# A two-layer decoder with a top-2 expert layer: experts ordered by size on the chip, the two smallest with both halves of 64 tokens side by side

## The chip, the cores and the metric

The kernel runs on one core of a Trainium2 chip. The metric is the device time of one execution in microseconds (us). The kernel before took 1534.06 us, the median of 3 runs (1532.68 to 1534.2). The engines are named as in the profile: PE (matrix products), PEld (its weight loads), DVE (vector), ACT (scalar), POOL (GpSimd) and SP, whose queue issues the DMAs that bring the weights.

## The reference, cut to what matters

256 tokens of width 1024 pass two layers. Each has a mixer (attention and a short convolution side by side), a feed-forward part and a gated embedding. The feed-forward part is dense in layer 0; in layer 1 every token goes to the two best of eight experts:

```python
def swiglu(x, w1, w3, w2):
    return (jax.nn.silu(x @ w1) * (x @ w3)) @ w2

logits = (xt @ router_w).astype(jnp.float32)
top_vals, top_idx = lax.top_k(logits, TOP_K)
gates = jax.nn.softmax(top_vals, axis=-1)
...
for e in range(N_EXPERTS):
    out = out + combine[:, e:e + 1] * swiglu(xt, w1[e], w3[e], w2[e])
```

An expert's w1 and w3 are 1024 x 3584, its w2 is 3584 x 1024, all fp32. With the inputs given, experts 0 to 7 get 53, 69, 62, 74, 73, 57, 68 and 56 tokens.

## The kernel before

**Precision.** An fp32 operand is split into a high part (a cast to the matrix format) and a low part (the rest). A product of two split operands is three products, low by high, high by low and high by high, summed in one PSUM tile (`mm3`, L180 to L183).

**Weights.** They come in DMAs of 1 MB, 128 partitions by 2048, into raw buffers (`load`, L82 to L86; 14 buffers, tag `raw`). `split` (L88 to L96) makes of each piece of PART = 1024 columns a high part `wh` (ACT, L94) and a low part `wl` (DVE, L95); there are NPART = 5 buffers for each. `prepare` splits ahead of use, `loads` issues DMAs ahead of that, and `weights` hands the parts to PE in the order of `plan`. A split can start when PE has used up a buffer of the five; a DMA when DVE has read a raw buffer.

**The expert layer** takes the time from 514 to 1499.5 us. `Route` computes the logits, ranks them by small DVE operations (L731 to L747) and numbers the tokens of each expert. `Gather` picks an expert's tokens (up to 128) by products with a 0/1 matrix `sl` (L809), two experts at a time, then scales them by the norm's gain and splits them (`scaled_split`, L210 and L211). Each expert goes through NB = 7 blocks of 512 hidden columns. In a block, `expert_up` makes two tiles `pe` of 128 tokens by 512 (48 products), ACT applies the Silu (`s`, L848), DVE multiplies (`m`, L851), `hidden_T` transposes `m` on PE (L586) and splits it into `th` (ACT, L590) and `tl` (DVE, L591), and `expert_down` adds 24 products to the two tiles `y`, one block later. So a block has six DMAs of weights, twelve pieces and 72 products of 512 columns. At an expert's end `y` is split (L877, L878) and `combine` brings it back to the tokens by products `pc` (L885, L886), which DVE adds, weighted with the gate, in two halves (L887). If an expert has more than 128 tokens, a second part of the program (`over`) runs after; it doesn't here.

**Order.** The order of PE's instructions is written out by hand everywhere, that of ACT and DVE too within the expert layer. An engine that waits holds up all that stands behind it.

The products of the second layer's embedding (`ppp`, 24 of them) stand in the last expert, in block EMB = 2.

Of the kernel before, what the change touches and what calls it, by code (L numbers as in the profile page):

```python
# [7 lines left out]
F32 = mybir.dt.float32  # L8
# [13 lines left out]
NE = 8  # L22
# [3 lines left out]
PART = 1024  # L26
NPART = 5
LOADS = (9, 14)
EMB = 2
EPS = 1e-6  # L30

# [13 lines left out]
def trunk(ctx: ExitStack, tc: tile.TileContext, a, out):  # L45
# [4 lines left out]
    rawp = pool("rawp", 14)  # L50
# [46 lines left out]

    def emb(l):

        return [(a["pT"][l].rearrange("p k s -> p (k s)"), S), (a["w_p"][l], D)]  # L100
# [3 lines left out]
    for l in range(2):  # L104
        plan += [(a["w_in"][l, j, hf], 512 if j < 3 else S) for j in range(6) for hf in range(2)]
        plan += [(a["w_o"][l, n, i], 512) for i in range(2) for n in range(2)]
        for e in range(1 if l == 0 else NE):
            up = [a[n] if l == 0 else a[n][e] for n in (("d_w1", "d_w3") if l == 0 else ("m_w1", "m_w3"))]
            dn = a["d_w2"] if l == 0 else a["m_w2"][e]
            plan += [[(w[b, hf], 512) for w in up for hf in range(2)] + [(dn[b, hf], D) for hf in range(2)]  # L110
                     + (emb(l) if (l, e, b) in ((0, 0, NB - 2), (1, NE - 1, EMB - 1)) else [])
                     for b in range(NB)]
        plan += [(a["w_g"][l, n, hf], 512) for n in range(2) for hf in range(2)]
# [19 lines left out]
    def loads(upto):  # L133

        for i in range(len(ready), min(upto, len(parts))):
            (src, n), c = parts[i]
            if i not in raws:
                w = src.shape[-1]
                raw = load(src, w, 2 if i < 4 else 1)
# [78 lines left out]
    class Transposed:  # L218
# [19 lines left out]
        def rest(self):  # L238
            self.step(4)
            self.step(6)  # L240
            if ahead[0] < NPART:
                ahead[0] = NPART
                prepare(used[0] - 2 + NPART)
# [63 lines left out]
    def mixer(l, xt, after):  # L307

        with tc.tile_pool(name="att", bufs=2) as ap, tc.tile_pool(name="att1", bufs=1) as a1:
            if l == 0:  # L310
# [5 lines left out]
                ready.extend([wp.tile([P, 2, 512], F32R, tag=n, name=n) for n in ("wh", "wl")] for _ in range(2))  # L316
# [5 lines left out]
                for k in range(KD):  # L322
                    scaled_split(xh[:, k, :], xl[:, k, :], xr[:, k, :], par[:, G_MIX + k:G_MIX + k + 1])
                    if k < 4:
                        wh, wl = [x[:, k % 2, :] for x in ready[k // 2]]
# [257 lines left out]
    def hidden_T(m, fp):  # L583
# [3 lines left out]
        th = fp.tile([P, 4, P], F32R, tag="th", name="th")  # L587
        tl = fp.tile([P, 4, P], F32R, tag="tl", name="tl")
# [77 lines left out]
    class Parts:  # L666


        def __init__(self):
            self.x = {}  # L670
# [5 lines left out]
        def part(self, n, t):  # L676
            self.half(n)
            hh, hl = self.x[n][:, 0, t, :], self.x[n][:, 1, t, :]
            hn = h[t][:, n * 512:(n + 1) * 512]
            nc.scalar.copy(hh, hn)  # L680
            nc.vector.tensor_sub(hl, hn, hh.bitcast(F32))

        def block(self, k, t):

            return [self.x[k // 4][:, i, t, k % 4 * P:(k % 4 + 1) * P] for i in (1, 0)]

    class Route:


        def __init__(self, l):  # L690
            self.l = l
            self.rs = TokenRstd()
            self.split = Parts()
# [31 lines left out]
        def choose(self, mp, rp):  # L725
# [22 lines left out]

            pp = tp.tile([P, 512], F32, tag="t", name="ppos")
# [454 lines left out]
```

## Time and profile before

| what | us |
|---|---|
| median of 3 runs | 1534.06 |
| the profiled execution | 1535.4 |
| its span | 1533.4 |
| PE busy | 1512.3 (99%) |
| DVE busy | 1280.8 (84%) |
| ACT busy | 1093.1 (71%) |
| DMA, share of 16 engines' span | 76.3% |

The span is the profiled execution from its first to its last instruction; 2.0 us lie around it. Busy PE says that a product was under way or queued in the array, not that it ran at full rate: products overlap, so the distance between the starts of two is what one costs, not the length of its row.

### The profile page before, as it was taken

The page shows a single profiled execution, that of the slowest core. Times are in us where ns is not written, and L with a number is a line of the kernel's source. Part 1 is how long each engine was busy: PE and PEld are TensorE (multiplying, and loading weights), DVE is VectorE, ACT ScalarE, POOL GpSimd, SP SyncE. Part 2 cuts the span into 40 slices and gives each one's busy share as a digit, 9 for nine tenths or more (in the row PEclk, how much of TensorE's full clock was granted, in tenths as well). Part 3 has the DMA queues.
Part 4 walks back from the last instruction along what each step waited for, and adds up shares of the span by engine and source line. Part 5 has one row for each costly group of instructions (what it writes and reads, how often), then busy time and mean ns, then how long its engine had stood idle before and what let it go on. Part 6 is the DMA issues. An engine that isn't in the chain of part 4 may idle for free.

```text
span 1533.4 us, 19945 instructions
## 1 busy us (share of the span) xinstructions
PE 1512.3 (99%) x7249; PEld 1255.3 (82%) x7249; DVE 1280.8 (84%) x1553; ACT 1093.1 (71%) x1470; POOL 92.7 (6%) x96
## 2 busy tenths in 40 slices
PE   7999999999999999999999999999999999999998
PEld 5888888887898788888888888888888888888886
DVE  6896555556788799999899899999999999999895
ACT  4756444446676678878878778777877887877874
POOL 3440000000242000000000000000000000000000
PEclk9999999999999899999999999999999999999999
DMA  9656555343444799897999998999998899989960
GB/s 360 253 208 231 192 192 171 138 164 111 169 186 168 284 378 352 329 357 283 361 375 370 356 362 329 380 398 378 356 358 333 312 359 380 375 335 338 355 264 30
DMA packets 64043, 445.84 MB, mean 291 GB/s; under 512 B 7104, under 2 KB 9024, under 8 KB 10432
## 3 DMA queue, kind: packets, MB, share of 16 engines
q1 hardware_dynamic: 63936, 444.48, 76.3%
q8 instruction: 59, 0.97, 0.2%
q14 instruction: 48, 0.39, 0.1%
HBM read 443.40 MB, written 1.05 MB: 290 GB/s over the span
## 4 chain that ended last, share of the span: by engine, by line
PE 93%; DVE 3%; ACT 1%; POOL 1%; DMA 1%; issue 1%; SPq 0%; DVEq 0%; ACTq 0%
PE pe L181 13%; PE pe L183 13%; PE pe L182 13%; PE y L183 8%; PE y L182 8%; PE y L181 8%; PE p L182 3%; PE p L183 3%; PE p L181 3%; PE pt L586 2%; PE pj L181 1%; PE pj L183 1%; PE pj L182 1%; DVE wl L95 1%; PE pg L809 1%; PE po L181 1%
## 5 line engine op out<-in xcount | busy, mean ns | idle before, releaser
L95 DVE TENSOR_TENSOR wl<-raw,wh 128x1024 fp32r<-128x1024 f32 (+1 forms) x999 | 1016.2, 1057 | 178.8 <-ACT wh L94 166.4
L94 ACT CAST wh<-raw 128x1024 fp32r<-128x1024 f32 (+1 forms) x1000 | 881.1, 913 | 238.0 <-PE pe L183 78.2
L181 PE MATMUL pe<-wh,xl 128*128 128x512 f32 x896 | 350.6, 391 | 0.0
L183 PE MATMUL pe<-wh,xh 128*128 128x512 f32 x896 | 349.2, 390 | 0.0
L182 PE MATMUL pe<-wl,xh 128*128 128x512 f32 x896 | 348.7, 389 | 0.0
L181 PE MATMUL y<-wh,tl 128*128 128x512 f32 x560 | 226.2, 404 | 0.0
L182 PE MATMUL y<-wl,th 128*128 128x512 f32 x560 | 220.8, 394 | 0.5 <-DVE wl L95 0.5
L183 PE MATMUL y<-wh,th 128*128 128x512 f32 x560 | 220.9, 394 | 0.0
L183 PEld LDWEIGHTS pe<-wh,xh 128*128 128x128 f32 x896 | 168.2, 188 | 36.3
L182 PEld LDWEIGHTS pe<-wl,xh 128*128 128x128 f32 x896 | 168.2, 188 | 35.9 <-DVE wl L95 0.4
L181 PEld LDWEIGHTS pe<-wh,xl 128*128 128x128 f32 x896 | 168.2, 188 | 35.1
L183 PEld LDWEIGHTS y<-wh,th 128*128 128x128 f32 x560 | 105.1, 188 | 25.2
L182 PEld LDWEIGHTS y<-wl,th 128*128 128x128 f32 x560 | 105.3, 188 | 22.7 <-DVE wl L95 1.2
L181 PEld LDWEIGHTS y<-wh,tl 128*128 128x128 f32 x560 | 105.3, 188 | 21.6 <-ACT wh L94 0.2
L181 PE MATMUL p<-wh,xl 128*128 128x512 f32 x224 | 87.8, 392 | 0.0
L183 PE MATMUL p<-wh,xh 128*128 128x512 f32 x224 | 87.3, 390 | 0.0
L182 PE MATMUL p<-wl,xh 128*128 128x512 f32 x224 | 87.2, 389 | 0.0
L590 ACT CAST th<-pt 128x512 fp32r<-128x512 f32 x70 | 40.9, 586 | 41.8 <-PE pt L586 41.8
L95 POOL TENSOR_TENSOR wl<-raw,wh 128x1024 fp32r<-128x1024 f32 x1 | 2.4, 2380 | 990.2 <-ACT wh L94 990.2
L181 PE MATMUL pu<-xh,wl 128*128 128x256 f32 x192 | 55.7, 290 | 0.0
L182 PE MATMUL pu<-xl,wh 128*128 128x256 f32 x192 | 54.3, 283 | 0.0
L183 PE MATMUL pu<-xh,wh 128*128 128x256 f32 x192 | 54.2, 283 | 0.0
(201 smaller groups left out, 1545.2 us busy)
## 6 DMA issues: line engine op xcount, KB each, us to landing
raw<-m_w SPq DMA_DIRECT2D x336, 1024.0 KB, 6.0
raw<-d_w SPq DMA_DIRECT2D x42, 1024.0 KB, 4.8
raw<-w_in SPq DMA_DIRECT2D x22, 1024.0 KB, 6.7
raw<-w_o SPq DMA_DIRECT2D x8, 1024.0 KB, 5.2
raw<-w_g SPq DMA_DIRECT2D x8, 1024.0 KB, 4.8
raw<-w_p SPq DMA_DIRECT2D x2, 1024.0 KB, 4.8
raw<-w_in SPq DMA_DIRECT2D x4, 256.0 KB, 5.0
raw<-w_in SPq DMA_DIRECT2D x2, 512.0 KB, 8.5
```

What stands on the lines that cost most here:

```text
L94: nc.scalar.copy(wh[:, cs], raw[:, cs])
L95: eng.tensor_sub(wl[:, cs], raw[:, cs], wh[:, cs].bitcast(F32))
L181: nc.tensor.matmul(ps, ll, rh, start=start, stop=False)
L182: nc.tensor.matmul(ps, lh, rl, start=False, stop=False)
L183: nc.tensor.matmul(ps, lh, rh, start=False, stop=stop)
L586: nc.tensor.transpose(pt[:, c * P:(c + 1) * P], m[:, c * P:(c + 1) * P], ident)
L590: nc.scalar.copy(th, pv)
L809: nc.tensor.matmul(pts[kk], src, self.sl[:, t, :, :].rearrange("p i s -> p (i s)"), start=(i == 0), stop=(i == 2 * NT - 1))
```

## The change

**Sizes.** A piece is now 2048 columns (a whole DMA), with 3 buffers for `wh` and `wl` in place of 5 of half the size, and 13 raw buffers in place of 14.

**Order of the experts.** Expert 0 goes first as before. `places` ranks the other seven by their count of tokens, with some 26 small DVE operations in the first block, and loads the order into registers of SP; the weights of places 1 to 7 are fetched from an address that a register gives (`expert_w`). Positions, selections and gates are brought into the same order (`by`). Here 56 and 57 tokens are the two smallest; they take places 2 and 5.

**Two small experts.** They have 64 slots. The high part of 64 tokens and their low part stand side by side in one stationary operand of 128 columns (`xs`). An up tile then takes two products per slice, by `wl` and by `wh` (L932), in place of three. Its partitions 0 to 63 then hold the high parts' share, 64 to 127 the low parts'; ACT copies the tile to SBUF (`f`, L938), and `fold` adds the two by one product with a matrix `both` (L945, fp32 on both sides, 64 x 512). The down part takes two products too (L986, L987); its halves are added in `combine`, where `iota2` gives both halves a slot. Each small expert runs with a large one, block by block in turn (`SETS`).

**Transposes.** Those of a block come in the next step: on PE after the first up piece (`turn`), DVE's low part after the second (`low`), behind `back`, which brings a finished expert to the tokens.

**Gathers.** h is scaled by the gain and split once (`gains`, `part`), then high and low parts are gathered separately and ACT alone takes them out of PSUM. The embedding's products go into the route (`fill`). The experts' results are added to h itself.

On PE, the end of an up part and the start of a down part; `pe` is the up tile, `y` the down tile, `xh` and `xl` the tokens. Before, any block:

```order
L181 MATMUL pe<-wh,xl 128x512
L182 MATMUL pe<-wl,xh 128x512
L183 MATMUL pe<-wh,xh 128x512
L181 MATMUL y<-wh,tl 128x512
L182 MATMUL y<-wl,th 128x512
L183 MATMUL y<-wh,th 128x512
```

After, a small expert's up part and the large one's down part behind it:

```order
L932 MATMUL pe<-wl,xs 128x512
L932 MATMUL pe<-wh,xs 128x512
L945 MATMUL pf<-f,both 64x512
L206 MATMUL y<-wh,tl 128x512
L207 MATMUL y<-wl,th 128x512
L208 MATMUL y<-wh,th 128x512
```

The up tile gets its second of two products where it got its third of three, and the fold's product stands between it and the down part.

On ACT, blocks of the expert layer; `th` is the transposed hidden tile's high part. Before, two blocks:

```order
L94 CAST wh<-raw 128x1024 x6
L590 CAST th<-pt 128x512
L94 CAST wh<-raw 128x1024 x6
L848 ACTIVATE s<-pe,rslot 128x512
L94 CAST wh<-raw 128x1024 x6
```

After, one step of a small and one of a large expert (the first Silu, `s<-pf`, is the small one's):

```order
L101 CAST wh<-raw 128x2048 x5
L972 CAST th<-pt 128x512
L101 CAST wh<-raw 128x2048
L938 COPY f<-pe 128x512
L101 CAST wh<-raw 128x2048 x2
L938 COPY f<-pe 128x512
L952 ACTIVATE s<-pf,rslot 64x512
L101 CAST wh<-raw 128x2048 x3
L972 CAST th<-pt 128x4x64
L101 CAST wh<-raw 128x2048
L952 ACTIVATE s<-pe,rslot 128x512
```

Half as many casts of twice the width, and two copies `f` between those of the small expert.

On DVE, the end of one expert and the start of the next; the numbers tell tiles apart. Before:

```order
L878 TENSOR_TENSOR y_6081<-y_5147,y_6081 128x512
L878 TENSOR_TENSOR y_6081<-y_5148,y_6081 128x512
L95 TENSOR_TENSOR wl_6090<-raw_6087,wh_6089 128x1024
L95 TENSOR_TENSOR wl_6100<-raw_6087,wh_6099 128x1024
L95 TENSOR_TENSOR wl_6112<-raw_6109,wh_6111 128x1024
L95 TENSOR_TENSOR wl_6122<-raw_6109,wh_6121 128x1024
L887 SCALAR_TENSOR_TENSOR hout_6133<-pc_6134,gate_4953,h0_97 128x512
L887 SCALAR_TENSOR_TENSOR hout_6133<-pc_6138,gate_4953,h1_98 128x512
L95 TENSOR_TENSOR wl_6146<-raw_6143,wh_6145 128x1024
L95 TENSOR_TENSOR wl_6156<-raw_6143,wh_6155 128x1024
L887 SCALAR_TENSOR_TENSOR hout_6133<-pc_6165,gate_4953,h0_97 128x512
L887 SCALAR_TENSOR_TENSOR hout_6133<-pc_6169,gate_4953,h1_98 128x512
```

After:

```order
L1008 TENSOR_TENSOR y_5640<-y_4798,y_5640 128x512
L1008 TENSOR_TENSOR y_5640<-y_4799,y_5640 128x512
L102 TENSOR_TENSOR wl_5649<-raw_5646,wh_5648 128x2048
L102 TENSOR_TENSOR wl_5679<-raw_5676,wh_5678 128x2048
L1017 SCALAR_TENSOR_TENSOR h0_97<-pc_5692,gatev_4583,h0_97 128x512
L1017 SCALAR_TENSOR_TENSOR h1_98<-pc_5696,gatev_4583,h1_98 128x512
L978 TENSOR_TENSOR tl_5700<-pt_5660,th_5665 128x512
L102 TENSOR_TENSOR wl_5706<-raw_5703,wh_5705 128x2048
L1017 SCALAR_TENSOR_TENSOR h0_97<-pc_5717,gatev_4583,h0_97 128x512
L1017 SCALAR_TENSOR_TENSOR h1_98<-pc_5721,gatev_4583,h1_98 128x512
```

Two casts' worth of `wl` still stand between the split of `y` and the first add, and the low part `tl` of the hidden tile `pt_5660`, transposed before, now comes behind the adds of `pc_5692` and `pc_5696`. The pool `tp` has two PSUM tiles for `pt` and `pc`.

The diff, cut to its core:

```diff
-PART = 1024
-NPART = 5
-LOADS = (9, 14)
-EMB = 2
+PART = 2048
+NPART = 3
+LOADS = (9, 10)
+HALF = 64
+SETS = ((0,), (1, 2), (3,), (4, 5), (6,), (7,))
+SMALL = (2, 5)
+RANK = (0, 3, 1, 4, 5, 2, 6, 7)
+STEPS = [(e, b) for es in SETS for b in range(NB) for e in es]
...
-    rawp = pool("rawp", 14)
+    rawp = pool("rawp", 13)
...
+    chosen = {}
+    class expert_w:
+        def __init__(self, name, e, b, hf):
+            self.at, self.shape = (name, e, b, hf), (P, 2048)
+
+        def ap(self):
+            name, e, b, hf = self.at
+            if e == 0:
+                return a[name][0][b, hf]
+            return a[name][bass.ds(chosen[e], 1), b, hf].rearrange("o p n -> (o p) n")
...
+        def gains(self):
+            self.g = rawp.tile([P, 2 * D], F32, tag="raw", name="gain")
+            for n in range(2):
+                pt = tp.tile([P, 512], F32, tag="t", name="pgn")
+                for k in range(4):
+                    nc.tensor.matmul(pt[:, k * P:(k + 1) * P],
+                                     par[:, self.g0 + n * 4 + k:self.g0 + n * 4 + k + 1].broadcast_to([P, P]), ident,
+                                     start=True, stop=True)
+                nc.scalar.copy(self.g[:, n * 512:(n + 1) * 512], pt)
...
+            ns = slice(n * 512, (n + 1) * 512)
+            hg = self.g[:, D + t * 512:D + (t + 1) * 512]
+            nc.vector.tensor_mul(hg, h[t][:, ns], self.g[:, ns])
+            nc.scalar.copy(hh, hg)
+            nc.vector.tensor_sub(hl, hg, hh.bitcast(F32))
...
+            fill()
...
+        def places(self):
...
+            nc.vector.tensor_copy(c8, self.n8)
+            nc.vector.memset(c8[:, 0:1], -1.0)
+            nc.vector.tensor_tensor(same, row(c8), col(c8), op=ALU.is_equal)
+            nc.vector.tensor_mul(same, same, elow)
+            nc.vector.tensor_tensor(less, row(c8), col(c8), op=ALU.is_lt)
+            nc.vector.tensor_add(less, less, same)
+            rank = rp.tile([P, NE], F32, tag="rank8", name="rank8")
+            nc.vector.reduce_sum(rank, less, axis=AX.X)
+            nc.vector.tensor_tensor(at, row(rank), col(self.q8), op=ALU.is_equal)
+            nc.vector.reduce_sum(order, tmp, axis=AX.X)
+            self.order = mp.tile([P, NE], I32, tag="orderi", name="orderi")
+            nc.vector.tensor_copy(self.order, order)
...
+            for e in range(1, NE):
+                chosen[e] = nc.values_load(self.order[0:1, e:e + 1], engines=[mybir.EngineType.SP],
+                                           min_val=0, max_val=NE - 1)
...
+            self.x = xp.tile([P, KD, S], F32R, tag=tag, name="xe")
+            if self.n > 1:
+                self.xs = rawp.tile([P, KD, P], F32R, tag="raw", name="xs")
+
+        def step(self, k, pls=((tp, "t"), (tp, "t"))):
+            w = P + (self.n - 1) * HALF
+            for kk, (pl, tag) in enumerate(pls):
+                pt = pl.tile([P, 512], F32, tag=tag, name="pg")
+                for i in range(2):
+                    for t in range(NT):
+                        nc.tensor.matmul(pt[:, i * w:(i + 1) * w], self.rt.split.block(k + kk, t)[i],
+                                         self.sl[:, t, :, :].rearrange("p i s -> p (i s)")[:, 0:w],
+                                         start=(t == 0), stop=(t == NT - 1))
+                pv = pt[:, 0:2 * w].rearrange("p (i s) -> p i s", i=2)
+                nc.scalar.copy(self.x[:, k + kk, :].rearrange("p (i s) -> p i s", i=2), pv[:, :, 0:P])
+                if self.n > 1:
+                    nc.scalar.copy(self.xs[:, k + kk, :].rearrange("p (i s) -> p i s", i=2), pv[:, :, P:w])
 
...
-                mm3(st[j], g.h[:, kk, ts], g.l[:, kk, ts], *w(k),
-                    start=(kk == 0), stop=(kk == KD - 1))
+                if i:
+                    for n, x in enumerate(reversed(w(k))):
+                        nc.tensor.matmul(st[j], g.xs[:, kk, :], x, start=(kk == n == 0), stop=(kk == KD - 1 and n == 1))
+                else:
+                    mm3(st[j], g.x[:, kk, 0:P], g.x[:, kk, P:S], *w(k), start=(kk == 0), stop=(kk == KD - 1))
             if hf == 1:
-                if j == 0:
-                    st["s"] = fp.tile([P, 512], F32, tag="s", name="s")
-                    nc.scalar.activation(st["s"], st[0], AF.Silu, scale=rk())
+                if i:
+                    st["f", j] = fp.tile([P, 512], F32, tag="f", name="f")
+                    nc.scalar.copy(st["f", j], st[j])
                 else:
-                    st["m"] = fp.tile([P, 512], F32, tag="m", name="m")
-                    nc.vector.scalar_tensor_tensor(st["m"], st[1], rk(), st["s"], op0=ALU.mult, op1=ALU.mult)
+                    out(j)
+        def fold(j):
+
+            st[j] = mm.tile([P, 512], F32, tag="mm", name="pf")
+            nc.tensor.matmul(st[j][0:HALF], g.rt.both, st["f", j], start=True, stop=True)
+            out(j)
...
+    def expert_T(m, small, fp):
+        def turn():
+            pt = tp.tile([P, 512], F32, tag="t", name="pt")
+            for c in range(4):
+                nc.tensor.transpose(pt[:, c * n:(c + 1) * n], m[0:n, c * P:(c + 1) * P], ident[0:n, 0:n])
+            th = fp.tile([P, 4, P], F32R, tag="th", name="th", bufs=1)
+            pv = pt[:, 0:4 * n].rearrange("p (c q) -> p c q", q=n)
+            nc.scalar.copy(th[:, :, 0:n], pv)
+        def low():
+            pv, th = st
+            tl = th[:, :, HALF:P] if small else fp.tile([P, 4, P], F32R, tag="tl", name="tl", bufs=1)
+            nc.vector.tensor_sub(tl, pv, th[:, :, 0:n].bitcast(F32))
...
+    def down_mms(ps, ht, c, wh, wl, start, stop):
+        th, tl = ht
+        if tl is None:
+            nc.tensor.matmul(ps, th[:, c, :], wl, start=start, stop=False)
+            nc.tensor.matmul(ps, th[:, c, :], wh, start=False, stop=stop)
+        else:
+            mm3(ps, th[:, c, :], tl[:, c, :], wh, wl, start=start, stop=stop)
...
+            fill[0]()
...
+            rt.choose(self.m1, self.m1, lambda: run(fill[1:3]))
+            fill[3]()
+            g = self.gather(0)
...
-            for e in range(NE):
-                for b in range(NB):
-                    up, st = expert_up(None, b, g[e // 2], e % 2, lambda: sT[e][1], mp)
-                    pe_, pb = (e, b - 1) if b else (e - 1, NB - 1)
-                    dn = expert_down(None, pb, lambda: ht, ys[pe_]) if pe_ >= 0 else ()
+                combine(h, h, yp[e], sT[e][0], lambda t: rt.by["gate"][:, t, e:e + 1], n, **where)
+
+            for i, es in enumerate(SETS):
+                steps = [(e, b) for b in range(NB) for e in es]
+                        if ht is None:
+                            turn, ht = expert_T(pst["m"], pe_ in SMALL, mp)
+                    final = (i, j) == (len(SETS) - 1, len(steps) - 1)
+                    last = len(steps) - j
                     up[0]()
+                    if turn:
+                        turn[0]()
...
+                    if (i, j) == (0, 0):
+                        rt.places()
                     up[1]()
-                    if b == 1 and e:
-                        back(e - 1, 0)
+                    for x in now:
+                        back(x, 0)
+                    if turn:
+                        turn[1]()
                     up[2]()
-                    if b == 1 and e:
-                        back(e - 1, 1)
...
                     up[3]()
+                    if small:
+                        st["fold"](0)
+                    if prev:
                         dn[0]()
+                    if small:
+                        st["fold"](1)
                         dn[1]()
-                        if (e, b) == (NE - 1, EMB):
-                            for f in fill:
-                                f()
                         if pb == NB - 1:
                             y_split(ys[pe_], yp[pe_], 0)
                             y_split(ys[pe_], yp[pe_], 1)
+                            todo.append(pe_)
+                    prev = (e, b, st)
```

## Rows read from the trace of the kernel before

**Rows 1.** The page, parts 1 and 4: busy time by engine; engines on the last chain.
```profile
PE 1512.3 (99%) x7249; PEld 1255.3 (82%) x7249; DVE 1280.8 (84%) x1553; ACT 1093.1 (71%) x1470; POOL 92.7 (6%) x96
...
PE 93%; DVE 3%; ACT 1%; POOL 1%; DMA 1%; issue 1%; SPq 0%; DVEq 0%; ACTq 0%
```

**Rows 2.** Table by stretch: span; PE, PEld, DVE, ACT, POOL busy; clock, DMA share, GB/s.
```profile
514.00:1499.50 985.50, 985.27 (x4484) 810.00 (x4482) 908.80 (x886) 780.38 (x858) 0.00 (x0) 1.00 0.91 349
...
1000.00:1100.00 100.00, 100.00 (x451) 82.12 (x451) 93.32 (x88) 79.24 (x86) 0.00 (x0) 1.00 0.97 382
```

**Rows 3.** Instructions by line and form, PE: busy, mean ns; idle before, releaser.
```profile
L182 PE MATMUL y<-wl,th 128*128 128x512 f32 x560 | 220.8, 394 | 0.5 <-DVE wl L95 0.5
```

**Rows 4.** Waits of the queues that issue DMAs: us in total, times, longest.
```profile
SPq L85 <- DVE wl L95: 1122.2, 359, 17.2
```

**Rows 5.** Timeline around the end of an up part: start, us, engine, line.
```profile
800.08 0.39 PE L181 MATMUL pe<-wh,xl 128*128 128x512 f32 x1
...
800.76 0.40 PE L181 MATMUL y<-wh,tl 128*128 128x512 f32 x1
...
800.96 1.05 ACT L94 CAST wh<-raw 128x1024 fp32r<-128x1024 f32 x1 [0.30 <-PE pe L183]
...
803.33 0.40 PE L183 MATMUL y<-wh,th 128*128 128x512 f32 x1
...
803.92 0.48 PE L181 MATMUL y<-wh,tl 128*128 128x512 f32 x1
```

**Rows 6.** Instructions by line and form, DVE and ACT.
```profile
L95 DVE TENSOR_TENSOR wl<-raw,wh 128x1024 fp32r<-128x1024 f32 x678 | 801.2, 1222 | 69.0 <-ACT wh L94 57.6 <-DMA raw<-m_w 2.6
L94 ACT CAST wh<-raw 128x1024 fp32r<-128x1024 f32 x679 | 700.3, 1053 | 120.7 <-PE pe L183 77.9 <-PE y L183 30.6 <-DVE wl L95 2.4
...
L95 DVE TENSOR_TENSOR wl<-raw,wh 128x512 fp32r<-128x512 f32 x319 | 214.2, 712 | 109.9 <-ACT wh L94 108.8
L94 ACT CAST wh<-raw 128x512 fp32r<-128x512 f32 x319 | 180.1, 618 | 117.1 <-PE p L183 59.5 <-PE y L183 42.2 <-PE pj L183 5.8
...
L591 DVE TENSOR_TENSOR tl<-pt,th 128x512 fp32r<-128x512 f32 x70 | 48.1, 689 | 1.5 <-ACT th L590 1.3
...
L851 DVE SCALAR_TENSOR_TENSOR m<-pe,rslot,s 128x512 f32<-128x512 f32 x56 | 41.8, 746 | 0.0
L590 ACT CAST th<-pt 128x512 fp32r<-128x512 f32 x70 | 40.9, 586 | 41.8 <-PE pt L586 41.8
```

**Rows 7.** Timeline of ACT and DVE, a cast and the subtract it releases.
```profile
808.39 1.05 ACT L94 CAST wh<-raw 128x1024 fp32r<-128x1024 f32 x1 [0.34 <-PE pe L183]
809.47 3.95 DVE L95 TENSOR_TENSOR wl<-raw,wh 128x1024 fp32r<-128x1024 f32 x3 [0.17 <-ACT wh L94]
```

**Rows 8.** Timeline of PE around products of whole fp32 operands.
```profile
70.11 0.65 PE L476 MATMUL po<-tt,vg 128*64 128x256 f32 x4
70.60 0.39 PE L479 MATMUL po<-tt,vg 128*64 128x128 f32 x4
```

**Rows 9.** Timeline of PE, half of one gather step pair.
```profile
745.49 2.07 PE L809 MATMUL pg<-sl,hx 128*128 128x256 f32 x16
747.40 0.40 PE L181 MATMUL y<-wh,tl 128*128 128x512 f32 x1
```

**Rows 10.** Timeline of an expert's return to the tokens, one half.
```profile
651.59 0.39 PE L885 MATMUL pc<-y,slT 128*128 128x512 f32 x1
...
652.50 0.39 PE L181 MATMUL pe<-wh,xl 128*128 128x512 f32 x1
...
653.10 1.41 DVE L887 SCALAR_TENSOR_TENSOR hout<-pc,gate,h 128x512 f32<-128x512 f32 x2
```

**Rows 11.** The route: table by stretch, then timeline of DVE and PE.
```profile
507.00:514.00 7.00, 5.86 (x35) 5.81 (x36) 5.36 (x17) 2.87 (x7) 1.61 (x1) 0.59 0.23 68
...
506.91 0.17 DVE L746 TENSOR_SCALAR selb<-rank 128x16 bf16<-128x16 f32 x1
...
507.15 0.19 PE L751 MATMUL ppos<-selb,bits 128*128 128x8 bf16 x1 [1.92 <-DVE selb L746]
```

More of the change, by code (lines that the diff above doesn't have):

```diff
@@ L315, in mixer @@
                 xr = rawp.tile([P, KD, S], F32, tag="raw", name="xr")
-                ready.extend([wp.tile([P, 2, 512], F32R, tag=n, name=n) for n in ("wh", "wl")] for _ in range(2))
+                ready.append([wp.tile([P, 4, 512], F32R, tag=n, name=n) for n in ("wh", "wl")])
                 src = plan[0][0].rearrange("p (k n) -> p k n", n=512)
@@ L580, in mixer, with hidden_T @@
             return nxt
-    def hidden_T(m, fp):
+    def hidden_T(m, fp=None):
         pt = tp.tile([P, 512], F32, tag="t", name="pt")
@@ L895, in __init__, with gather, route @@
         def __init__(self, rt, m1, mp):
[L896 to L904 removed]
+            self.rt, self.m1, self.mp, self.out = rt, m1, mp, h
+            rt.both = m1.tile([P, HALF], F32, name="both")
+            nc.gpsimd.tensor_add(rt.both, ident[:, 0:HALF], ident[:, HALF:P])
+            rt.iota2 = m1.tile([P, P], F32, name="iota2")
+            for n in range(2):
+                nc.gpsimd.tensor_copy(rt.iota2[:, n * HALF:(n + 1) * HALF], iota[:, 0:HALF])
+            rt.q8 = m1.tile([P, NE], F32, name="q8")
+            for e, q in enumerate(RANK):
+                nc.gpsimd.memset(rt.q8[:, e:e + 1], float(q))
+        def gather(self, i):
+            rt = self.rt
+            by = rt.by if i else {"pos": rt.pos, "sel": rt.sel}
+            return Gather(rt, by["pos"], by["sel"], [slice(e, e + 1) for e in SETS[i]], self.mp, ("xl", "xh")[i % 2])
+        def route(self, fill):
+            rt = self.rt
             n = len(ready)
@@ L921, in route, with main @@
             rt.rs.done()
-            prepare(n + 2)
+            prepare(n + 1)
             for i, k in enumerate(range(0, KD, 2)):
-                g.step(k, *((acc, "acc") if i % 2 else (tp, "t")), apart=True)
+                g.step(k, ((acc, "acc"),) * 2 if i % 2 else ((tp, "t"),) * 2)
             rt.gates()
             return g
-        def main(self, first, fill):
+        def main(self, first):
             mp, rt = self.mp, self.rt
-            col = lambda e: slice(e, e + 1)
             g = {0: first}
@@ L967, in main @@
                     up[2]()
-                    if b == 1 and e:
-                        back(e - 1, 1)
+                    for x in now:
+                        back(x, 1)
                     up[3]()
-                    if more:
-                        if b == 4:
-                            g[e // 2 + 1] = self.pair(e // 2 + 1, split)
-                        elif b > 4:
-                            g[e // 2 + 1].step((b - 5) * 4)
-                            g[e // 2 + 1].step((b - 5) * 4 + 2)
@@ L1109, in trunk @@
             with tc.manual_schedule(engines={mybir.EngineType.Activation, mybir.EngineType.DVE}):
-                loads(len(ready) + 2 * LOADS[0])
-                late = moe.main(moe.route(), prep)
+                loads(len(ready) + LOADS[0])
+                late = moe.main(moe.route(prep))
                 ahead[0] = 3
```

230 lines of the change are left out of this document (121 added, 109 removed).

## The prediction

> **What bounds the kernel now.** I read the page first: PE is busy 99% of the span and holds 93% of the last chain [rows 1]. By stretch, the expert layer is 985.5 of the 1533.4 us, and there PE is busy 985.27, DVE 908.80 and ACT 780.38, at full clock [rows 2]. So PE sets the time, but DVE has only 8% to spare. PE's own waits are next to nothing: its one product that waited on DVE did so for 0.5 us in all [rows 3]. The DMA queue waits 1122 us for DVE to read raw buffers [rows 4]: weights lie ready before they are wanted. What is to be found is how much PE work goes, and whether DVE, ACT and the buffers between them still keep up.
>
> **PE work removed and added.** The timeline gives 0.227 us from one up product to the next (three from 800.08 to 800.76) and 0.234 for a down product (eleven from 800.76 to 803.33); four transposes take 803.92 - 803.33 - 0.23 = 0.36 [rows 5]. A block is 48 x 0.227 + 24 x 0.234 + 0.36 = 16.9.
> - Two experts have 7 blocks each that lose 16 up and 8 down products: 14 x (16 x 0.227 + 8 x 0.234) = -77.1.
> - 28 folds. No fp32 product 512 columns wide is in the trace; two of 256 columns (four records) take 70.60 - 70.11 = 0.49 [rows 8]. I take that, the same number of columns: 28 x 0.49 = +13.7. The bounds are half (half the records) and twice of it, -6.9 and +13.7.
> - The embedding's 24 products leave the expert layer: -5.4.
> - Gathers: 16 products of 256 columns take 1.91, 0.119 each [rows 9]; three gathers of 32 were 11.4. Five of 32, of 128 or 192 columns, at about 0.096 (between 0.06, in proportion to 128, and 0.119): 15.4. So +4.0.
>
> Together -64.8, if PE never waits. A row supports the fold's price against a rule. L476's two products show two records each. The Trainium skill ("FP8 and Floating Point Precision", TensorE Precision Notes) says that true fp32 takes four passes through the array; by that rule a fold would be near 0.9 and the sum an estimated 12 us higher, and the trace doesn't agree, with two records to a product.
>
> **The buffer round.** When PE leaves a weight buffer, ACT casts into it, DVE subtracts, and only then PE can use it again. From PE's last product to ACT 0.20 (800.76 to 800.96 [rows 5]); from ACT's end to DVE 0.03 (809.44 to 809.47 [rows 7]); from DVE's end to PE 0.07 (507.08 to 507.15 [rows 11]). A cast of 1024 columns is 1.053, of 512 0.618; a subtract 1.222 and 0.712 [rows 6]. Carried on at that slope, 2048 columns are 1.92 on ACT and 2.24 on DVE (bounds: no saving from joining two, 2.11 and 2.44; a tenth below, 1.73 and 2.02). The round was 0.20 + 1.05 + 0.03 + 1.22 + 0.07 = 2.57, against the four other pieces that PE had left, 4 x 1.36 = 5.4: slack 2.9. Now it is 0.20 + 1.92 + 0.03 + 2.24 + 0.07 = 4.46, against two pieces. Two large up pieces are 24 x 0.227 = 5.45, slack 1.0; two small ones 16 x 0.227 = 3.63 or 16 x 0.234 = 3.74, which is 0.7 to 0.8 short. This is where the cover goes.
>
> **A pair of blocks.** PE's work is 16.9 for the large one and 32 x 0.227 + 16 x 0.234 + 2 x 0.49 + 0.3 = 12.3 for the small one: 29.2. DVE has 12 x 2.24, two `m` of 0.75, a `tl` of 0.69 and one of half the width, some 0.4: 29.5. They are level, so DVE has nothing left to catch up with. The six small pieces come in a row (two down, four up): PE wants 2 x 1.87 + 4 x 1.82 + 0.36 = 11.4, DVE has 6 x 2.24 + 0.75 + 0.69 = 14.9. Walked piece by piece, each waiting for its round and for what stands ahead on ACT and DVE: first small up piece 0.72 by the round, 1.1 with `m` ahead on DVE; third 0.3; fourth 0.36 by the round, 1.1 with the copy `f` (0.59, as `th`) ahead on ACT; the two down pieces behind 0.5 and 0.1. That is 3.1 a pair, 14 x 3.1 = +43.4. The lower bound, with 2.02 and 1.73 or waits spread evenly, is DVE's work less PE's, 0.3 a pair (+4); the upper, with 2.44 and 2.11, is 5.2 a pair (+73).
>
> **Experts' ends.** `back` makes two tiles `pc`; the order shows `pt` still held, so the second `pc` waits for DVE to add the first, behind two subtracts. Counted from the last down product: ACT casts `y` twice, 0.20 + 2 x 0.59 = 1.38, then the third piece's cast to 3.30, `th` to 3.89, the fourth's cast to 5.81; DVE's subtract starts at 5.84 and ends at 8.08, the add (half of 1.41 [rows 10]) at 8.79, PE goes on at 8.86. PE itself is there at 2.72 + 0.36 + 2.72 + 0.46 = 6.26. It waits 2.6; queued behind it are all up products of the step. Seven ends: +18.2 (bounds 0, if DVE is a piece ahead, and 28). Before, both tiles were free: the next product followed at 652.50 while the adds ran at 653.10 [rows 10].
>
> **The rest.** `places` puts 26 small operations on DVE; seven such before `selb` held PE for 1.92 [rows 11], 0.27 each, so 7.0 in the first block, of which the round's slack and DVE's spare 0.5 a piece take half: +3.5 (0 to 7). The seven register loads stand on SP, ahead of DMAs, with nine to ten raw buffers in hand: 0. The route gains eight small products, two copies and four multiplications, and the embedding's products, 5.4 at full clock, more at the 0.59 granted there [rows 11], fill part of PE's 1.92 and later wait: +3 (-3 to +10). Layer 0 and the tail have PE work per piece at least as large as a large up piece: 0.
>
> **Sum.** -64.8 + 43.4 + 18.2 + 3.5 + 3 = +3.3. The profiled execution took 1535.4 (span 1533.4 and 2.0 around), 1.3 above the median, so 1535.4 + 3.3 - 1.3 = 1537.4; I say 1537. With all bounds low, -64.8 - 6.9 + 4 - 3 = -71 gives 1463; all high, -64.8 + 13.7 + 73 + 28 + 7 + 10 = +67 gives 1601.
>
> **Rivals.**
> - *B, the waits stay small.* DVE's subtract of 2048 a little under 2.24, and the round's late pieces partly covered by products already queued: 1.3 a pair (18), 1.2 an end (8), 4 for the rest: -64.8 + 30 = -35, 1500. For it: DVE and PE level on average. Against it: three buffers leave no way to carry slack from large pieces to small ones, and DMA. The expert layer drew 349 GB/s at a share of 0.91, and 382 at 0.97 in its densest stretch [rows 2]; a pair needs 12.6 MB, at 382 GB/s 32.9 us. Before it took 33.8, by my sum 32.3, here 30.5, which the raw buffers' lead can bear only in part.
> - *C, slower: joining two halves saves nothing on DVE.* The place is the run of small pieces; at 2.44 and 2.11 the round is 4.85, 1.1 to 1.2 short, and a pair waits 5.2 in place of 3.1, an end 3.4 in place of 2.6: +29 + 6, so 1572. It decides from about 2.35 for a subtract on. Against it: 512 columns cost more than half of 1024 in both engines [rows 6].
> - *D, slower by the clock.* Behind PE's waits in the route the granted clock was 0.59 for 7 us [rows 11], a mix of the levels 1.2 and 2.4 GHz. If each of seven ends brought as much, 7 x 7 x 0.41 = 20 more: 1557. Against it: 3.1 us a pair come in pieces of about 1 us, with dense work between. The Trainium skill ("TensorE: Matmul & The Clock Gate", HAM oscillation) tells of kernels whose waits for data send the clock down again and again; of waits of this length in dense work no row here shows a fall.
> - *E, it doesn't do what it says:* a small expert with more than 64 tokens would start the second part. The counts are 56 and 57: 1 in 100.
>
> **How the numbers follow.** A (the sum) has 0.52, with 1520 to 1554 as its own range; B 0.27, C 0.15, D 0.05, E 0.01. Range 1499 to 1563: it takes in most of B and the near part of C and D. A difference within 0.2%, 3.1 us, can't be told from none. Faster: all of B and 0.15 of A, 0.42. Same: 0.12 of A, 0.12. Slower: 0.25 of A and the rest, 0.46.
>
> **What would show it.** Right: the 2048 subtract near 2.24 and cast near 1.92; PE idle about 3 us a pair, at the first and fourth small up piece, released by DVE's `wl`; about 2.6 at the second `pc` of each expert; no wait in single experts' blocks; folds 0.49 apart. Wrong: PE still busy 99% in pairs (B); a subtract over 2.35 (C); a clock under 1.00 past the first block (D); DVE waiting for raw buffers by more than the 2.6 us of before [rows 6], which would make DMA the bound.

## The result, and the profile after

The changed kernel takes 1569.91 us (median of 4 runs, 1567.82 to 1573.95) against 1533.37 of the kernel before in the same session. The ratio is 1.0243, with a 95% interval of 1.0231 to 1.0256: slower by 36.5 us. The profiled execution took 1573.95, its span is 1572.2.

The page again, busy time by engine and the last chain, beside [rows 1]:

```profile
PE 1507.9 (96%) x7049; PEld 1206.8 (77%) x7049; DVE 1213.8 (77%) x1040; ACT 1034.1 (66%) x1022; POOL 96.0 (6%) x107
...
PE 81%; DVE 8%; ACT 5%; issue 4%; POOL 1%; DMA 0%; SPq 0%; ACTq 0%; DVEq 0%
```

PE is busy about as long as before (1507.9), but its share of the chain fell from 93% to 81%, and DVE and ACT now have 13% of it. So its busy time hardly fell, though fewer products are left (7049 for 7249), and waits came on top: busy time also holds late starts and products at a lower clock. The expert layer (from the first up product to the first return of the last expert), and then 160 us within the first pair of experts; columns as in [rows 2]:

```profile
522.80:1537.30 1014.50, 974.98 (x4241) 756.95 (x4241) 861.37 (x535) 736.82 (x567) 0.00 (x0) 0.98 0.90 341
680.00:840.00 160.00, 152.90 (x637) 110.92 (x637) 136.68 (x78) 121.86 (x87) 0.00 (x0) 1.00 0.96 372
```

The layer is 1014.5 us long where it was 985.4 (514.3 to 1499.65): +29. The route before it begins the first up product at 522.8 instead of 514.3: +8.5. The tail is 1 longer. In the pair PE stands 7 of 160 us.

The lines that answer to [rows 6], and the small experts' first product of each slice:

```profile
L102 DVE TENSOR_TENSOR wl<-raw,wh 128x2048 fp32r<-128x2048 f32 x339 | 769.3, 2289 | 140.9 <-ACT wh L101 139.5
L101 ACT CAST wh<-raw 128x2048 fp32r<-128x2048 f32 x340 | 647.2, 1912 | 144.5 <-PE y L208 72.3 <-PE pe L208 63.3 <-PE pe L932 8.7
...
L932 PE MATMUL pe<-wl,xs 128*128 128x512 f32 x224 | 94.1, 420 | 19.2 <-DVE wl L102 19.2
```

The joined pieces cost 2.29 on DVE and 1.91 on ACT; I had said 2.24 and 1.92. What PE waited for in the expert layer (us in total, times, longest):

```profile
PE pe L932 <- DVE wl L102: 19.2, 24, 0.9
PE pc L1015 <- DVE h L1017: 16.6, 7, 2.9
PE pe L207 <- DVE wl L102: 3.7, 3, 3.0
```

These are the waits that were forecast: 24 at small up pieces, seven of 2.0 to 2.9 us at the experts' ends, one of 3.0 in the first block. They don't cost their length alone. Behind each of the seven ends the granted clock falls: over 5 us from about the second `pc` on it is 0.66 in all seven, a mix of the levels 2.4 and 1.2 GHz. The first and the last, columns as above:

```profile
674.00:679.00 5.00, 5.00 (x16) 3.92 (x16) 4.92 (x5) 1.90 (x1) 0.00 (x0) 0.66 0.60 224
1432.00:1437.00 5.00, 4.96 (x15) 3.93 (x16) 3.55 (x3) 0.00 (x0) 0.00 (x0) 0.66 0.71 265
```

That is 5 x 0.34 = 1.7 us an end, an estimate of 12 us in seven. In the pair above the clock is 1.00. One pair step in PE's timeline:

```profile
737.72 0.50 PE L932 MATMUL pe<-wl,xs 128*128 128x512 f32 x1 [0.73 <-DVE wl L102]
...
745.07 0.50 PE L932 MATMUL pe<-wl,xs 128*128 128x512 f32 x1 [0.83 <-DVE wl L102]
...
747.12 1.07 PE L945 MATMUL pf<-f,both 128*64 128x512 f32 x2
748.13 0.50 PE L206 MATMUL y<-wh,tl 128*128 128x512 f32 x1
...
751.12 1.07 PE L945 MATMUL pf<-f,both 128*64 128x512 f32 x2
752.12 0.50 PE L206 MATMUL y<-wh,tl 128*128 128x512 f32 x1
...
771.24 0.50 PE L932 MATMUL pe<-wl,xs 128*128 128x512 f32 x1 [0.72 <-DVE wl L102]
```

It runs from 737.72 to 771.24, 33.5 us, of which I had forecast 32.3. There are two waits (before the first and the fourth small piece). The folds take 748.13 - 747.12 = 1.01 and 752.12 - 751.12 = 1.00, twice what I had put down.

### The profile page after: what moved, and what is told of

Read it like the earlier page. It is cut to its first block, busy times and chain, and to the rows that moved or that the text cites. A ratio compares the mean times of both kernels' runs of the same rounds, so it can differ in the third digit from the quotient of the medians.

```text
span 1572.2 us, 18819 instructions
## 1 busy us (share of the span) xinstructions
PE 1507.9 (96%) x7049; PEld 1206.8 (77%) x7049; DVE 1213.8 (77%) x1040; ACT 1034.1 (66%) x1022; POOL 96.0 (6%) x107
## 4 chain that ended last, share of the span: by engine, by line
PE 81%; DVE 8%; ACT 5%; issue 4%; POOL 1%; DMA 0%; SPq 0%; ACTq 0%; DVEq 0%
PE pe L206 9%; PE pe L207 9%; PE pe L208 9%; PE y L206 7%; PE y L207 7%; PE y L208 7%; DVE wl L102 6%; ACT wh L101 5%; PE pe L932 4%; PE p L208 3%; PE p L206 3%; PE p L207 3%; PE pf L945 2%; PE pg L898 2%; PE pt L969 1%
## 5 line engine op out<-in xcount | busy, mean ns | idle before, releaser
L102 DVE TENSOR_TENSOR wl<-raw,wh 128x2048 fp32r<-128x2048 f32 (+1 forms) x501 | 961.5, 1943 | 257.7 <-ACT wh L101 256.3
L101 ACT CAST wh<-raw 128x2048 fp32r<-128x2048 f32 (+1 forms) x502 | 808.3, 1628 | 277.2 <-PE y L208 115.6
L206 PE MATMUL pe<-wh,xe 128*128 128x512 f32 x672 | 270.8, 403 | 0.0
L207 PE MATMUL pe<-wl,xe 128*128 128x512 f32 x672 | 266.8, 397 | 3.7 <-DVE wl L102 3.7
L208 PE MATMUL pe<-wh,xe 128*128 128x512 f32 x672 | 266.5, 397 | 0.0
L206 PE MATMUL y<-wh,tl 128*128 128x512 f32 x440 | 177.4, 403 | 0.2 <-ACT wh L101 0.2
L208 PE MATMUL y<-wh,th 128*128 128x512 f32 x440 | 173.4, 394 | 0.0
L207 PEld LDWEIGHTS pe<-wl,xe 128*128 128x128 f32 x672 | 129.0, 192 | 32.1 <-DVE wl L102 5.3
L208 PEld LDWEIGHTS pe<-wh,xe 128*128 128x128 f32 x672 | 128.8, 192 | 28.2
L206 PEld LDWEIGHTS pe<-wh,xe 128*128 128x128 f32 x672 | 128.9, 192 | 27.3
L932 PE MATMUL pe<-wl,xs 128*128 128x512 f32 x224 | 94.1, 420 | 19.2 <-DVE wl L102 19.2
L932 PE MATMUL pe<-wh,xs 128*128 128x512 f32 x224 | 89.4, 399 | 0.0
L932 PEld LDWEIGHTS pe<-wl,xs 128*128 128x128 f32 x224 | 42.6, 190 | 42.6 <-DVE wl L102 34.7
L972 ACT CAST th<-pt 128x512 fp32r<-128x512 f32 (+1 forms) x55 | 29.3, 533 | 65.9 <-PE pt L969 65.9
```

The source lines that it names most:

```text
L101: nc.scalar.copy(wh[:, cs], raw[:, cs])
L102: eng.tensor_sub(wl[:, cs], raw[:, cs], wh[:, cs].bitcast(F32))
L206: nc.tensor.matmul(ps, ll, rh, start=start, stop=False)
L207: nc.tensor.matmul(ps, lh, rl, start=False, stop=False)
L208: nc.tensor.matmul(ps, lh, rh, start=False, stop=stop)
L932: nc.tensor.matmul(st[j], g.xs[:, kk, :], x, start=(kk == n == 0), stop=(kk == KD - 1 and n == 1))
```

## The experiments

All times are medians, the ratios against the kernel before on the same chip (1533 to 1534.5 in these sessions); gains are counted from the change's 1569.91. P is the theory that PE's instructions and the waits add up place by place; D that DVE's work and the buffer rounds set a pair's length whatever PE does; R that three buffers leave a round too little time; M that memory is the limit.

**The fold in one pass.**

```diff
-            rt.both = m1.tile([P, HALF], F32, name="both")
+            rt.both = m1.tile([P, HALF], F32R, name="both")
...
-                    st["f", j] = fp.tile([P, 512], F32, tag="f", name="f")
+                    st["f", j] = fp.tile([P, 512], F32R, tag="f", name="f")
```

> Part changed: the fold's two operands are of the matrix format, so the copied tile is rounded to it and the product is done in one pass. Theory P (the price of the fold on PE adds to the time): a fold goes from 1.00 us between starts to about 0.3, 28 of them, so 1570 - 20 = 1550. Theory D (the pair is held by DVE and the buffer rounds, the fold fills time that PE would wait anyway): the two waits of a pair, now 0.7 and 0.8 us, grow by most of what the folds lose, and the time is 1562 to 1570.

Measured 1544.31, ratio 1.0057 (1.004 to 1.0074): 26 us less than the change. PE's timeline around a fold, and PE's waits in the layer:

```profile
744.83 0.39 PE L945 MATMUL pf<-f,both 128*64 128x512 f32 x1
745.06 0.39 PE L206 MATMUL y<-wh,tl 128*128 128x512 f32 x1
```

```profile
PE pe L932 <- DVE wl L102: 19.2, 24, 0.9
PE pc L1015 <- DVE h L1017: 16.5, 7, 2.9
...
PE y L207 <- DVE wl L102: 1.8, 8, 0.2
```

A fold now is one record, 0.23 from the next product, and the waits of before are what they were. Of the 28 x 0.77 = 22 us only 1.8 came back, in eight short waits at down pieces. D falls. That 26 went and not 20 has no experiment of its own; in this run's profile the clock falls behind four of the seven ends, not all.

**The return in quarters.**

```diff
                     for x in now:
-                        back(x, 0)
+                        back(x, 0, ts=(0,))
...
                     for x in now:
-                        back(x, 1)
+                        back(x, 0, ts=(1,))
                     up[3]()
+                    for x in now:
+                        back(x, 1, ts=(0,))
...
                         dn[0]()
+                    for x in now:
+                        back(x, 1, ts=(1,))
```

> An expert's return to the tokens is issued in four parts, one behind each of four pieces, instead of two and two, so that no second tile waits for the add of the first. Theory P (the seven waits of 2.0 to 2.9 us add to the time): 1570 - 17 = 1553. Theory D (DVE is late there by the split of y in any case): the wait moves to the next piece that needs a subtract, 1563 to 1569.

Measured 1547.86, ratio 1.0088 (1.0071 to 1.0104): 22 less. PE's waits in the layer:

```profile
PE pe L932 <- DVE wl L102: 19.2, 24, 0.9
...
PE pc L1015 <- DVE h L1017: 2.1, 2, 1.0
```

Seven waits of 16.6 us became two of 2.1, and the 24 small ones did not grow. P again, with some 7 us more than the waits alone (14.5). The clock accounts for the rest: behind all seven ends it now stays at 1.00, here at the last, where it had been 0.66.

```profile
1411.00:1416.00 5.00, 5.00 (x23) 4.08 (x22) 5.00 (x4) 3.56 (x2) 0.00 (x0) 1.00 0.84 290
```

The two waits left, of 1.0, bring no fall.

**Three products for every expert.**

```diff
-SETS = ((0,), (1, 2), (3,), (4, 5), (6,), (7,))
-SMALL = (2, 5)
+SETS = tuple((e,) for e in range(8))
+SMALL = ()
```

> All else of the change, without the two passes: every expert alone, 128 slots, three products, no folds, order by size kept. Theory P: the kernel before plus the route (8.5), the experts' ends (18), the first block (6), two more gathers less the embedding (5): 1570 to 1577, so that two passes brought about nothing. Theory D (the two passes are what hurts, the rest is harmless): at or below 1550.

Measured 1587.29, ratio 1.0341 (1.0324 to 1.0359): slower than both theories said. So small experts in two passes, run in pairs and with two gathers fewer, do bring time, 17 us, and it is the rest of the change that costs 53. In its trace the route is 9 longer, the ends cost 18, the gathers 13 (28 steps of about 0.88 against 12 of 0.95 before), the first block with its half clock 9 and slow starts behind the transposes 5; less the embedding's 5.5, that is 49. This leaves out the clock behind the ends, which falls in five of seven; at 1.7 each that is more than the remaining 4, so some of the terms are a little large.

**Four buffers.**

```diff
-NPART = 3
-LOADS = (9, 10)
+NPART = 4
+LOADS = (8, 6)
...
-    rawp = pool("rawp", 13)
+    rawp = pool("rawp", 11)
```

> Four weight buffers of 2048 columns in place of three; 11 raw buffers in place of 13 make the room, and two loads fewer run ahead at the route. Theory R (three buffers leave a round too little time): the 24 waits of about 0.8 us at the small expert's pieces go, with their restarts, and part of the experts' ends: 1570 - 24 to 30, 1540 to 1546. Theory D (DVE's own work, 31 us a pair, is the limit): the waits stay, 1565 or more. Theory M (12.6 MB a pair at 382 GB/s): a pair goes from 33.5 to 32.9 at best, 1560 or more, DVE waits for DMAs.

With 12 raw buffers in place of 11 it did not fit: the pool `att` needs 21 KB a partition, and 18.2 were left. Measured 1538.94, ratio 1.0037 (1.0023 to 1.0051): 31 less. PE's waits in the layer, and the same 160 us:

```profile
PE pc L1015 <- DVE h L1017: 17.3, 7, 2.9
PE pt L969 <- DVE s L955: 2.3, 1, 2.3
PE pe L207 <- DVE wl L102: 1.1, 1, 1.1
```

```profile
680.00:840.00 160.00, 160.00 (x688) 120.49 (x687) 147.06 (x83) 130.74 (x96) 0.00 (x0) 1.00 0.99 395
```

All 24 waits at small pieces are gone and PE is busy throughout the pair, at 395 GB/s. R holds, 1 us past the upper of its gains; D and M fall. A pair is 31.0 us: this is PE's own work with folds of 1.0, where I had counted 29.2. The seven ends still wait.

**The halves added on POOL.**

```diff
-                    st["f", j] = fp.tile([P, 512], F32, tag="f", name="f")
-                    nc.scalar.copy(st["f", j], st[j])
+                    st["f", j] = fp.tile([HALF, 512], F32, tag="f", name="f")
+                    lo = fp.tile([HALF, 512], F32, tag="lo", name="lo", bufs=1)
+                    nc.scalar.copy(st["f", j], st[j][0:HALF])
+                    nc.scalar.copy(lo, st[j][HALF:P])
+                    nc.gpsimd.tensor_add(st["f", j], st["f", j], lo)
...
-            st[j] = mm.tile([P, 512], F32, tag="mm", name="pf")
-            nc.tensor.matmul(st[j][0:HALF], g.rt.both, st["f", j], start=True, stop=True)
+            st[j] = st["f", j]
```

> The two halves are added on POOL, not by a product: ACT copies partitions 0 to 63 and 64 to 127 of the up tile to the same 64 partitions (two copies of 0.59 in place of one), POOL adds them (about 1.2 us, half of its 2.38 for 1024 columns). Theory P (the fold's 1.0 us on PE adds to the time): 28 x 1.0 and two restarts of 0.1 each less, 1570 - 33 = 1537, or less gain by ACT's 28 copies. Theory D: the casts come later behind the copies and DVE shares with POOL, waits grow, 1555 to 1570.

Measured 1549.77, ratio 1.011 (1.0093 to 1.0127): 20 less, between the two. The addition (nanoseconds, shortest, median, longest):

```profile
L941 POOL TENSOR_TENSOR f<-f,lo x28: 1342/2324/3012, 673.5 to 1245.4; 64x512 f32<-64x512 f32 x28
```

It takes 2.3 us in the middle, not 1.2. Also DVE's subtract is a little longer beside it (2.31). And waits came that the change had next to none of:

```profile
PE y L207 <- DVE wl L102: 7.6, 8, 1.0
```

**The kernel before with the new sizes alone** (2048 columns, 3 and 13 buffers, and the counts of pieces that go with them).

```diff
-PART = 1024
-NPART = 5
-LOADS = (9, 14)
+PART = 2048
+NPART = 3
+LOADS = (9, 10)
...
-    rawp = pool("rawp", 14)
+    rawp = pool("rawp", 13)
```

> The kernel before with only the sizes changed: 2048 columns a piece, three buffers, 13 raw buffers. Theory P (large blocks keep 1.0 us of slack, so the size of a piece costs nothing there): 1532 to 1540, blocks 16.9 to 17.0 us. Theory R: the splits that stand for gathers and experts' ends use the slack up, and the time is 1545 or more.

Measured 1547.57, ratio 1.0096 (1.0079 to 1.0113): 15 slower than the 1532.8 of the kernel before beside it, in R's range. Blocks without anything else in them stay at 16.95 us. PE's waits in the layer:

```profile
PE pe L182 <- DVE wl L95: 5.9, 8, 1.8
PE ppp L182 <- DVE wl L95: 1.8, 1, 1.8
```

The kernel before had next to none [rows 3]. They stand where a gather's DVE operations or the embedding come between the splits: seven waits of 0.58 or 0.59 (one of them in the first block), and two of 1.8 at the embedding. The layer as a whole is 10 us longer. So the sizes cost, and not in the blocks that I had looked at.

**The route with the split early.**

```diff
+            rt.split.part(1, 0)
+            rt.split.part(1, 1)
             rt.choose(self.m1, self.m1, lambda: run(fill[1:3]))
+            rt.counts()
             fill[3]()
             g = self.gather(0)
-            rt.split.part(1, 0)
-            rt.split.part(1, 1)
             loads(n + LOADS[1])
-            rt.counts()
```

> In the route the split of h's second half comes before the ranking, as in the kernel before, and the copy of the counts, which frees the PSUM tile that the gather waits for, right behind it. Theory C (PE's wait of 3.7 us there costs itself and, with the clock at 0.50 for the 10 us behind it, about 5 more): 1570 - 4 to 9 = 1561 to 1566. Rival: the four operations delay the ranking by as much, and PE waits for that: 1568 to 1572.

Measured 1570.69, ratio 1.0253 (1.0236 to 1.027): no difference from the change. PE there:

```profile
514.26 0.19 PE L796 MATMUL ppos<-selb,bits 128*128 128x8 bf16 x1 [4.15 <-DVE selb L790]
...
517.12 2.08 PE L898 MATMUL pg<-sl,hx 128*128 128x128 f32 x10
```

The wait before the gather is gone, and one as long stands before the ranks' products. The rival holds: DVE's chain in the route is what lasts, in either order.

**Quarters and one pass together**, with three buffers (both diffs above).

> Three buffers of 2048; the return in quarters and the fold in one pass (its operands rounded) together. Theory P (each cure takes away time on PE or a wait that nothing refills): 1570 - 26 - 22 = 1522. Theory D: the experts' ends lean on the same subtracts as the small pieces, and 1530 or more comes out.

Measured 1524.14, ratio 0.9937 (0.9921 to 0.9954). P to 2 us: the two gains of 26 and 22 add up.

**Four buffers and quarters** (both diffs above).

> Four buffers of 2048 with 11 raw buffers, and the return in quarters; the fold as in the change. Theory R: 1570 - 31 - 22 = 1517, faster than the kernel before; a pair 31.0 us, ends without the wait. Theory M (memory at 395 GB/s in the pairs is full): the pairs stay at 31.0 but the ends no longer let the raw buffers fill again, DVE waits for DMAs, 1525 or more.

Measured 1515.19, ratio 0.9876 (0.9859 to 0.9893). R, to 2 us; a pair stays 31.0, at 399 GB/s, and M falls.

**Four buffers, quarters and one pass.**

> As the four buffers with quarters, and the fold in one pass (its operands rounded). Theory P (the fold's price on PE adds to the time also here): another 28 x 0.7 less, 1497. Theory D (with four buffers a pair is at DVE's own 31 us): a pair stays at 30.5 to 31, and 1510 to 1517 comes out. Theory M: the pair stays at 31.0 as well, but with DVE waiting for DMAs.

Measured 1489.66, ratio 0.9712 (0.9696 to 0.9728), the fastest of all, 80 us under the change and 44 under the kernel before. A fold's price comes off in full (25.5). 200 us of its first pair and around:

```profile
660.00:860.00 200.00, 198.91 (x904) 159.82 (x903) 193.60 (x113) 171.02 (x132) 0.00 (x0) 1.00 1.00 412
```

It is 7 less than P said, and D and M fall: a pair is 29.3 us. PE is still busy 99%, DVE 97%, and the DMA engines all the time at 412 GB/s. So little is left in any of the three; which comes next no run shows. Its fold rounds the copied tile to the matrix format, so part of the precision of the others is given up.

**Six buffers of half the size** (PART = 1024, NPART = 6, with the counts of pieces that go with them).

> The change with pieces of 1024 columns and six buffers, the same space as three of 2048. Theory R (what hurts is that a third of the buffers is held by one round): the round is 2.57 again against five pieces of about 1, the waits of 0.8 go, 1545 to 1550, a pair near 32 us. Theory D (DVE's time for a DMA's columns counts: 2 x 1.22 in place of 2.29, 1.9 a pair): 32.9 us a pair on DVE, 1560 or more.

Measured 1532.66, ratio 0.9991 (0.998 to 1.0003): 37 less than the change, more than R said, and level with the kernel before. A pair takes 31.0 as with four large buffers, though DVE has two subtracts where it had one. So the space was not short. More buffers and a shorter round came together here, and the run doesn't tell them apart.

**Four buffers, quarters, the addition on POOL.**

> Four buffers, the return in quarters, and the two halves added on POOL in full fp32 (two copies on ACT, one addition on POOL, no product). Theory P (PE's time and the waits add up): the fold's 1.0 us goes from PE, 28 times with its restarts: 1515 - 30 = 1485. Rival: POOL's addition took 1.3 to 3.0 us with three buffers, longer than two copies leave, and the casts behind the copies come later, so that a third of the gain comes back as waits: 1490 to 1500.

Measured 1511.88, ratio 0.986 (0.9844 to 0.9877): 3 less than with the folds on PE, which the two intervals don't tell apart, where P said 30 and the rival 15 to 25. The addition as above, and PE's largest wait in the layer:

```profile
L941 POOL TENSOR_TENSOR f<-f,lo x28: 1282/2764/8464, 670.6 to 1216.4; 64x512 f32<-64x512 f32 x28
```

```profile
PE pt L971 <- DVE s L957: 14.6, 9, 2.9
```

POOL's addition takes up to 8.5 us, DVE's `s` that needs it comes late, and PE waits for that up to 2.9 us at the transposes. All its waits in the layer are 25.9 us, against 6.3 with the folds on PE. Together with that run it is the fastest of the versions that keep the sum of the halves in fp32, 1.4% under the kernel before.

## Why the prediction was wrong

It said 1537, with 1563 as its upper end, and 1569.91 came. By its steps, with the profiled execution (forecast 1538.7, measured 1573.95, 35 more):

- **28 folds, +13.7: this is the step that failed.** They are 28 x 1.01 = 28.3, 14.6 more. I read 0.49 in [rows 8] as two products of 256 columns one behind the other and took it for one of 512. But L476 makes two heads' products, one to partitions 0 to 63 of its PSUM tile and one to 64 to 127, each with a stationary operand 64 columns wide. They ran side by side. In one place of the trace before, the second head's operand came late, and the first product stands alone: its row is 0.65 long, as long as that of both in [rows 8].

```profile
86.93 0.65 PE L476 MATMUL po<-tt,vg 128*64 128x256 f32 x2
87.83 0.43 PE L476 MATMUL po<-tt,vg 128*64 128x256 f32 x1 [0.26 <-POOL tt L468]
```

So 0.49 is the time of one, and twice as many columns take twice that. The trace after agrees with eight whole fp32 products of 128 columns (16 records), which take 496.06 - 494.36 = 1.70, or 0.85 for 512 columns:

```profile
494.36 1.95 PE L708 MATMUL pgn<-cst,par 128*128 128x128 f32 x16
496.06 0.48 PE L206 MATMUL po<-wh,xl 128*128 128x512 f32 x1
```

The rule that I had set against the row was the better one: the Trainium skill ("FP8 and Floating Point Precision", TensorE Precision Notes) counts four passes for true fp32, an estimated 0.9 us, and the trace after shows 1.00 to 1.01. The one-pass run bears the term out: 26 us went with the folds' extra time.
- **PE's other work in a pair.** With four buffers PE does not wait in a pair, and 31.0 is its own work, against 29.2. The folds make 1.0 of the difference. The other 0.8, some 11 us in 14 pairs, is slow starts, which the sum put at nothing: before and behind a fold or transposes a product starts 0.32 to 0.33 after the one before it, not 0.23, and there are more such changes in a small block than in a large one. (The kernel before had 2 of the 11 too: its blocks took 16.95 where I had 16.87.)
- **Waits in a pair, 3.1 forecast.** 33.5 - 31.0 = 2.5, and only 12 of the 14 steps have them (24 waits): 30, so 13 less in all. They stand at two of the five places that I had named (first and fourth piece), the third has 0.15, the two down pieces none: the longer folds lay before them.
- **Experts' ends, +18.2.** The waits are right in place and nearly in size, 16.6. The clock behind them, 12, is not in the sum, so the ends cost 29, 10 more. The quarters took 22 away. The rows of one end after are the ones that I had worked out:

```profile
669.76 0.40 PE L1015 MATMUL pc<-y,slT 128*128 128x512 f32 x1
...
670.26 2.29 DVE L102 TENSOR_TENSOR wl<-raw,wh 128x2048 fp32r<-128x2048 f32 x1 [0.28 <-ACT wh L101]
...
672.47 0.74 DVE L1017 SCALAR_TENSOR_TENSOR h<-pc,gatev,h 128x512 f32<-128x512 f32 x1
673.26 0.50 PE L1015 MATMUL pc<-y,slT 128*128 128x512 f32 x1 [2.88 <-DVE h L1017]
```

DVE is in the second of the two subtracts until 672.5, the add of the first `pc` stands behind it, and PE's second `pc` waits 2.88 us for that add.

- **The first block, +3.5:** a wait of 3.0, 2.5 for a half clock that I had counted to the route alone, and 1.7 for a second fall behind the wait: 4 more.
- **The route, +3.** It is 8.5. The embedding's products did fill PE's wait of 1.92 before `ppos`, which is gone. But a new wait comes: the gather needs DVE's split of h and the copy of the counts, which frees a PSUM tile. Table by stretch, then PE:

```profile
514.00:518.00 4.00, 0.78 (x6) 0.81 (x6) 2.33 (x6) 2.61 (x8) 0.00 (x0) 0.96 0.05 6
518.00:522.00 4.00, 4.00 (x21) 4.00 (x20) 0.64 (x5) 1.78 (x5) 0.70 (x1) 0.50 0.69 256
```

```profile
513.00 0.56 PE L898 MATMUL pg<-sl,hx 128*128 128x128 f32 x4
517.22 5.78 PE L898 MATMUL pg<-sl,hx 128*128 128x128 f32 x28 [3.67 <-DVE n L808]
522.80 0.73 PE L206 MATMUL pe<-wh,xe 128*128 128x512 f32 x1
```

PE waits 3.67 and does 0.78 of 4 us, and behind it the granted clock is 0.50, one of the two levels, 1.2 GHz, into the first block. Before it had been 0.59 over 7 us, with a wait of 1.92 [rows 11].
- **Gathers, +4:** +6. **Large blocks alone, 16.9:** 17.0, 1.4 in 28 of them. **Tail, 0:** +1.

The differences are 14.6 + 9 - 13 + 10 + 4 + 5.5 + 2 + 1.4 + 1 = 34.5 of 35. The fold is the largest term that was too small, but it doesn't explain the miss alone: 14.6 more would have been 1552, within the range. The slow starts and the clock behind the ends, both at nothing in the sum, did the rest, and the waits in a pair, forecast too long, hid part of it.

Of the rivals, B stood on waits that stay small, and they didn't. C has the price that came, but not for its reason: a subtract costs 2.29 and not 2.44. D is right in its mechanism at the places that it named, and I had given it 0.05: its sign, a clock under 1.00 past the first block, is there behind all seven ends, at 1.7 each and not 2.9. In the pairs, with waits of 0.7 to 0.9, it stayed at 1.00, as the argument against D said. What the prediction had right was that three joined buffers turn the cover of a round into waits, and for the most part where.

## What to carry to other kernels

Count what an added product costs from a row of the same shape that stands alone; two products with half-width operands that ran beside each other hid half the price here. When buffers are joined to save fixed costs, count how many pieces of PE's work remain for a round, at the shortest piece and at the places where other operations stand in the same queues: three of 2048 cost 15 us even without the rest of the change, while four of 2048 or six of 1024 took the waits from the small pieces. Waits in front of the engine that sets the time are worth removing one by one, and can cost more than their length: seven waits of 16.6 us in all brought 12 us of lower clock with them. Here the cures added up to within 2 us of 80.

## What the runs showed of the hardware

POOL's addition of two 64 x 512 tiles took 1.28 us at its shortest, 2.76 in the middle and 8.46 at its longest (four buffers, quarters, POOL). One long and one short addition, and DVE's subtracts of two SBUF operands around them:

```profile
727.75 6.68 DVE L102 TENSOR_TENSOR wl<-raw,wh 128x2048 fp32r<-128x2048 f32 x3
732.12 8.45 POOL L941 TENSOR_TENSOR f<-f,lo 64x512 f32<-64x512 f32 x1 [21.32 <-ACT lo L940]
734.95 4.47 DVE L102 TENSOR_TENSOR wl<-raw,wh 128x2048 fp32r<-128x2048 f32 x2
741.27 1.28 POOL L941 TENSOR_TENSOR f<-f,lo 64x512 f32<-64x512 f32 x1 [0.70 <-ACT lo L940]
743.65 2.29 DVE L102 TENSOR_TENSOR wl<-raw,wh 128x2048 fp32r<-128x2048 f32 x1 [4.22 <-ACT wh L101]
```

The short one ran while DVE stood idle, the long one beside subtracts for 7 of its 8.45 us. The Trainium skill ("GPSIMD Engine Reference", Specifications) names contention of POOL with such DVE instructions on their SBUF interface; the runs agree, and the price here is up to 7 us on one instruction.
